# Five load buffers for the expert weights, with transposed halves in shared buffers and both silus first

## The chip, the cores and the metric

The kernel runs on one core of one Trainium2 chip. The metric is the device time of one execution in microseconds; lower is better. The names used below are those of the profile: PE is TensorE (matmuls), ACT is ScalarE, DVE is VectorE, POOL is GpSimd, SP is SyncE, whose queue issues nearly all plain DMA transfers.

## What is computed

One layer of a diffusion backbone over 2048 tokens of 1024 channels: a gated short convolution, and then a mixture of 16 experts in which each expert chooses its own 256 tokens. Cut to the part that the change touches:

```python
def expert_choice_ffn(h, w_router, w_gate, w_up, w_down):
    cap = EC_CAPACITY_FACTOR * N // N_EXPERTS                       # 256
    aff = jax.nn.softmax((h @ w_router).astype(jnp.float32), axis=-1)
    g, idx = lax.top_k(jnp.swapaxes(aff, 1, 2), cap)
    xs = jax.vmap(lambda hb, ib: hb[ib])(h, idx)
    hid = jax.nn.silu(einsum('becd,edf->becf', xs, w_gate)) * einsum('becd,edf->becf', xs, w_up)
    ys = einsum('becf,efd->becd', hid, w_down) * g[..., None]
    # rows of ys are added to the output at idx
```

Everything is float32. The expert weights are 16 x 3 x 1024 x 1024 numbers, 201 MB, each read once.

## The kernel before

The convolution part takes the first 800 us or so, then the router and a first search for the thresholds of experts 0 and 1, and from about 857 us on the experts, which the change is about. All of it is one program written out in Python; each engine executes its own instructions strictly in the order in which they are written, and the kernel sets that order by hand.

**Weights.** They come in pieces of 512 KB (`pieces`, 128 partitions x 1024 numbers). `load_piece` (L181) takes a buffer of the tag `raw`, of which there are `n_raw` = 3, and issues the load on SP's queue. `split_high` copies the piece, rounded to TensorE's float32r, into the first half of a `ws` buffer on ScalarE (L200); `split_low` subtracts that from the piece into the second half, on VectorE (L210). With the low half done the `raw` buffer is free, and the load of the piece three places on is issued (`load_to(i + n_raw)`). There are eight `ws` buffers (`n_split`); one comes free when the matmuls have used it.

**Products.** Three matmuls make one product in float32 precision: high by high, high by low, low by high. `gate_up(e, fh)` computes one half of the hidden channels of expert `e` for the gate and the up weights (192 matmuls of 256 columns, L1047, L1049 and L1051, into four PSUM banks), in eight steps `k`; `between(k)` places other work in them. Its eviction is a silu on ScalarE (L1057), a multiply on VectorE (L1058), a copy to the high half of `hT` on ScalarE (L1060) and a subtraction for the low half on VectorE (L1061), for each of two pairs of banks. `down(e, dh)` computes half of the output channels (48 matmuls of 512 columns, L1069 to L1071, two banks, four steps `kk`), evicted at L1089 and added into the output by an indirect DMA (L1095). Six banks are shared in turn, so a `gate_up` waits for the eviction of the `gate_up` before it. The order over experts is `gate_up(e, 0)`, `down(e-1, 0)`, `gate_up(e, 1)`, `down(e-1, 1)`.

**The tokens of the next expert.** `pick_oh` builds one-hot masks on VectorE (`oh`), `pick` multiplies them to the list of token numbers and issues two row gathers on POOL (L987) into two `xs` buffers, 128 rows each, whose float32 numbers lie as two halves of 16 bits. `turn(e, s)` transposes the rows of one half of the tokens by a DMA on SP's queue (L1015) into `tr`. `join(e, s)` puts the 16-bit halves together in `full` (VectorE L1021, ScalarE L1022) and splits that into `xT`, high on ScalarE (L1025), low on VectorE (L1026). The next expert's first matmul needs all of `xT`. In the kernel before, both turns and both joins stand inside `gate_up(e, 1)`, at k = 1, 3 and 5, 7.

Of the kernel before, what the change touches and what calls it, by code (L numbers as in the profile page):

```python
# [7 lines left out]
F32 = mybir.dt.float32  # L8
# [3 lines left out]
U16 = mybir.dt.uint16  # L12
# [5 lines left out]
P = 128  # L18
D = 1024
L = 2048  # L20
E = 16
CAP = 256
KD = D // P
# [13 lines left out]
def dram(src, offset, ap):  # L37
    return bass.AP(tensor=src.tensor, offset=src.offset + offset, ap=ap)
# [3 lines left out]
def block_kernel(ctx: ExitStack, tc, x, c, ada_w, ada_b, norm_g, w_in, conv, w_out, router, wg, wu, wd, out):  # L42
# [3 lines left out]
    wpool = ctx.enter_context(tc.tile_pool(name="weights", bufs=1))  # L46
# [3 lines left out]
    n_raw, n_split = 3, 8  # L50
# [121 lines left out]
    pieces, n_load, n_high, n_done = [], 0, 0, 0  # L172
# [3 lines left out]
        pieces.append((src, offset, ap, shape))  # L176
        return len(pieces) - 1

    raws = {}

    def load_piece(i):  # L181
        src, offset, ap, shape = pieces[i]
        t = wpool.tile([P] + shape, F32, name="raw", tag="raw", bufs=n_raw)
        nc.sync.dma_start(t, dram(src, offset, ap))
        raws[i] = t

# [2 lines left out]
    def load_to(i):  # L189
        nonlocal n_load  # L190
        while n_load <= min(i, len(pieces) - 1, load_end[0] - 1):
            load_piece(n_load)
            n_load += 1
# [10 lines left out]
    def split_low(i, eng=None, part=0, n=1):  # L204
        nonlocal n_done
        split_high(i)
        t, raw = ws_of[i], raws[i]
        w = pieces[i][3][-1] // n
        s = slice(part * w, (part + 1) * w)
        (eng or nc.vector).tensor_sub(t[:, 1, ..., s], raw[..., s], t[:, 0, ..., s].bitcast(F32))  # L210
        if part == n - 1:
            raws.pop(i)
            n_done += 1
            load_to(i + n_raw)

    def split_to(i, eng=None):
        while n_done <= min(i, len(pieces) - 1):
# [737 lines left out]
    moe = ctx.enter_context(tc.tile_pool(name="moe", bufs=1, reuse_waits="tile"))  # L955
# [16 lines left out]
    def pick(e):  # L972
        oh, ax = oh_of.pop(e)
        pi = tp.tile([P, 2, 5], F32, name="pi", tag="tp")
        for b in range(NB):
            nc.tensor.matmul(pi, oh[:, b], ax[:, b], start=(b == 0), stop=(b == NB - 1))
        pk = small.tile([P, 2, 5], F32, name="pk", tag="pk", bufs=2)
        nc.vector.tensor_copy(pk, pi)
        idx = small.tile([P, 2], I32, name="idx", tag="idx", bufs=4)
        nc.vector.scalar_tensor_tensor(idx, pk[:, :, 1], float(P), pk[:, :, 0], op0=ALU.mult, op1=ALU.add)  # L980
        xs_of[e] = []
        for s in range(2):
            if e:
                xs, src = moe.tile([P, 2 * D], U16, name="xs", tag="xs", bufs=2), hhalf.rearrange("t h d -> t (h d)")
            else:
                xs, src = moe.tile([P, D], F32, name="xs", tag="xs", bufs=2), hscr
            nc.gpsimd.indirect_dma_start(  # L987
                out=xs, out_offset=None, in_=src,
                in_offset=bass.IndirectOffsetOnAxis(ap=idx[:, s:s + 1], axis=0))
            xs_of[e].append(xs)  # L990
        gate = small.tile([P, 2], F32, name="gate", tag="gate", bufs=4)
        nc.vector.tensor_add(gate, pk[:, :, 2], pk[:, :, 3])
        nc.vector.tensor_add(gate, gate, pk[:, :, 4])
        idx_of[e], gate_of[e] = idx, gate

    def fetch(e, i, bank=None):
        g, s = divmod(i, 2)
        if i == 0:
            xT_of[e] = moe.tile([P, 2, KD, CAP], F32R, name="xT", tag="xT", bufs=2)
        xT, xs = xT_of[e], xs_of[e][s]  # L1000
        pt = (bank or tp).tile([P, 4, P], F32, name="pt", tag="mm" if bank else "tp")
        for j in range(4):
            nc.tensor.transpose(pt[:, j], xs[:, (4 * g + j) * P:(4 * g + j + 1) * P], identf)
        d = (slice(None), slice(4 * g, 4 * g + 4), slice(s * P, (s + 1) * P))
        nc.scalar.activation(xT[:, 0][d], pt, AF.Copy)
        nc.vector.tensor_sub(xT[:, 1][d], pt, xT[:, 0][d].bitcast(F32))

    tr_of = {}

    def turn(e, s):  # L1010

        if s == 0:
            xT_of[e] = moe.tile([P, 2, KD, CAP], F32R, name="xT", tag="xT", bufs=2)
        tr = tr_of[e, s] = moe.tile([P, 2 * KD, P], U16, name="tr", tag="oh" if s else "tr", bufs=1)
        nc.sync.dma_start_transpose(tr, xs_of[e][s])  # L1015

    def join(e, s):
        tr = tr_of.pop((e, s)).rearrange("p (h k) t -> p h (k t)", h=2)
        full = moe.tile([P, KD * P], F32, name="full", tag="full", bufs=1)
        both = full.bitcast(U16).rearrange("p (n h) -> p h n", h=2)  # L1020
        nc.vector.tensor_copy(both[:, 0], tr[:, 0])  # L1021
        nc.scalar.activation(both[:, 1], tr[:, 1], AF.Copy)  # L1022
        f = full.rearrange("p (k t) -> p k t", t=P)
        hi, lo = (xT_of[e][:, i, :, s * P:(s + 1) * P] for i in range(2))
        nc.scalar.activation(hi, f, AF.Copy)  # L1025
        nc.vector.tensor_sub(lo, f, hi.bitcast(F32))  # L1026

    def gate_up(e, fh, between=lambda k: None):
        xT = xT_of[e]
        if fh == 0:  # L1030
            hT_of[e] = {}
        ps = [[mm.tile([P, 2, CAP], F32, name="pm", tag="mm") for _ in range(2)] for _ in range(2)]
        for kk in range(KD // 2):
            for j in range(2):
                k = 2 * kk + j
                n = w_moe[0, e, fh, kk] + n_split - 2 + j
                if (e, fh) != (0, 1):
                    split_high(n)
                between(k)
                while n_done <= min(n, len(pieces) - 1):  # L1040
                    split_low(n_done, nc.gpsimd if n_done % 2 and (e, fh) < (1, 1) else None)
                for f in range(4):
                    c0 = slice(f * P, (f + 1) * P)
                    for m in range(2):
                        o = ps[m][f // 2][:, f % 2]
                        w = ws_of[w_moe[m, e, fh, kk]]
                        nc.tensor.matmul(o, w[:, 0, j, c0], xT[:, 0, k], start=(k == 0 and f % 2 == 0), stop=False,  # L1047
                                         skip_group_check=True)
                        nc.tensor.matmul(o, w[:, 0, j, c0], xT[:, 1, k], start=False, stop=False,  # L1049
                                         skip_group_check=True)  # L1050
                        nc.tensor.matmul(o, w[:, 1, j, c0], xT[:, 0, k], start=False, stop=(k == KD - 1),  # L1051
                                         skip_group_check=True)
        hT = moe.tile([P, 2, 4, CAP], F32R, name="hT", tag="hT", bufs=4)
        hT_of[e][fh] = hT
        for f2 in range(2):
            sg = moe.tile([P, 2, CAP], F32, name="sg", tag="sg", bufs=2)
            nc.scalar.activation(sg, ps[0][f2], AF.Silu)  # L1057
            nc.vector.tensor_mul(sg, sg, ps[1][f2])  # L1058
            t = slice(2 * f2, 2 * f2 + 2)
            nc.scalar.activation(hT[:, 0, t], sg, AF.Copy)  # L1060
            nc.vector.tensor_sub(hT[:, 1, t], sg, hT[:, 0, t].bitcast(F32))  # L1061
# [44 lines left out]
    def tick(k):  # L1106
        next(rounds, None)
# [8 lines left out]
    pick_oh(1)  # L1116
    for i in (0, 2, 1, 3):
        fetch(0, i, mm)
    for e in range(E):
        if e == 0:  # L1120
            gate_up(0, 0, lambda k: (tick(k), pick(1) if k == 7 else None))
            gate_up(0, 1, lambda k: (tick(k), turn(1, k - 2)) if k in (2, 3) else join(1, k - 5) if k in (5, 6) else None)
            continue
        if e == 1:
            gate_up(1, 0, lambda k: tick(k) if k > 1 else None)
            down(0, 0, lambda kk: tick(kk) if kk else None)
            for _ in rounds:
                pass
            pick_oh(2)
            gate_up(1, 1, lambda k: pick(2) if k == 2 else turn(2, k - 6) if k > 5 else None)  # L1130
        else:
            if e + 1 < E:
                pick_oh(e + 1)
            gate_up(e, 0)
            down(e - 1, 0, (lambda kk: pick(e + 1) if kk == 1 else None) if e + 1 < E else (lambda kk: None))
            gate_up(e, 1, (lambda k: turn(e + 1, k // 2) if k in (1, 3) else join(e + 1, k // 2 - 2) if k in (5, 7) else None)
                    if e + 1 < E else (lambda k: None))
        if e == 1:
            down(e - 1, 1, lambda kk: join(2, kk - 1) if kk in (1, 2) else None)
        else:  # L1140
            down(e - 1, 1)
    down(E - 1, 0)
    down(E - 1, 1)

# [21 lines left out]
```

## Time and profile before

| | |
|---|---|
| median of 3 runs | 2000.06 us (1997.33 to 2007.17) |
| the profiled execution | 2000.56 us, span 1998.8 us |
| mean granted TensorE clock | 0.978 |
| PE busy | 94% of the span |
| DVE, ACT, POOL busy | 58%, 41%, 17% |
| DMA moved | 368.50 MB, mean 184 GB/s |
| the sixteen experts | from about 857 us to the end |

In the profile's rows the first number is a start in microseconds from the start of the span, the second a duration; a group's row ends with the idle time before it and what ended that idle time. A windows row gives the length of a stretch, then for each engine its busy time and its number of instructions, then the granted clock, the busy share of the DMA engines and GB/s. A waits row gives who waited for whom: total, times, longest. Line numbers are those of the kernel before. A matmul's recorded end is modelled, and consecutive ones overlap.

### The profile page before, as it was taken

The numbers are of one execution on the slowest core, as the hardware profiler recorded it, in microseconds if no ns is written. First come the engines' busy times: TensorE is split into PE (matmuls) and PEld (weight loads), VectorE is DVE, ScalarE is ACT, GpSimd is POOL, SyncE is SP. The second block draws the span as 40 slices with busy tenths as digits, with TensorE's granted clock in tenths as the row PEclk, the third lists the DMA queues.
The fourth block names the chain that finished last, engine by engine and source line by source line (L and its number), as shares of the span: only waits on it lengthen the run. The fifth ranks groups of instructions, "written<-read, shape, count | busy, mean of one in ns | idle before, by whom it ended". The sixth has DMA issues, their size and how long they took to land.

```text
span 1998.8 us, 29375 instructions
## 1 busy us (share of the span) xinstructions
PE 1885.4 (94%) x11690; PEld 1659.4 (83%) x11690; DVE 1151.3 (58%) x1656; ACT 820.8 (41%) x1066; POOL 343.7 (17%) x521
## 2 busy tenths in 40 slices
PE   4999999999999999289999999999999999999998
PEld 3788888888888888288899989889898988988896
DVE  7644435344346667877656665665665656566554
ACT  3421126111123444456444454554445445454442
POOL 3310011010112223433102102101200110211101
PEclk9999999999999999589999999999999999999999
DMA  9343241433245565346777878778677777867866
GB/s 283 124 148 132 69 142 51 150 136 117 69 132 173 190 196 190 137 140 194 210 237 218 214 220 247 207 220 234 203 223 229 232 216 223 239 197 229 244 203 155
DMA packets 281278, 368.50 MB, mean 184 GB/s; under 512 B 74748, under 2 KB 156724, under 8 KB 281140
## 3 DMA queue, kind: packets, MB, share of 16 engines
q1 hardware_dynamic: 265172, 308.94, 50.5%
q0 software_dynamic: 15968, 57.68, 10.8%
q8 instruction: 91, 1.49, 0.3%
q14 instruction: 47, 0.39, 0.1%
HBM read 300.51 MB, written 50.33 MB: 176 GB/s over the span
## 4 chain that ended last, share of the span: by engine, by line
PE 58%; DMA 14%; DVE 12%; issue 7%; ACT 6%; SPq 2%; POOL 1%; POOLq 0%; ACTq 0%; DVEq 0%
PE pm L439 8%; PE pm L440 8%; PE pm L442 8%; PE pm L1051 5%; PE pm L1047 5%; PE pm L1049 5%; DVE ws L210 4%; DMA raw<-in_moe_w_gate_dram 4%; DMA raw<-in_moe_w_down_dram 4%; ACT ws L200 3%; DMA raw<-in_moe_w_up_dram 3%; PE pm L644 3%; PE pm L647 3%; PE pm L645 3%; PE pm L1071 2%
## 5 line engine op out<-in xcount | busy, mean ns | idle before, releaser
L210 DVE TENSOR_TENSOR ws<-raw,ws 128x1024 fp32r<-128x1024 f32 x415 | 499.6, 1225 | 315.6 <-ACT ws L200 312.2
L200 ACT ACTIVATE ws<-raw 128x1024 fp32r<-128x1024 f32 x437 | 452.7, 1055 | 459.8 <-DMA raw<-in_moe_w_down_dram 202.0
L1047 PE MATMUL pm<-xT,ws 128*128 128x256 f32 x2048 | 580.1, 283 | 21.2 <-DVE sg L1058 14.7
L1049 PE MATMUL pm<-xT,ws 128*128 128x256 f32 x2048 | 575.2, 281 | 5.2 <-DVE xT L1026 4.9
L1051 PE MATMUL pm<-xT,ws 128*128 128x256 f32 x2048 | 574.2, 280 | 2.5 <-DVE ws L210 2.5
L1047 PEld LDWEIGHTS pm<-xT,ws 128*128 128x128 f32 x2048 | 392.1, 191 | 30.6 <-DVE sg L1058 19.3
L1049 PEld LDWEIGHTS pm<-xT,ws 128*128 128x128 f32 x2048 | 391.8, 191 | 9.0 <-DVE xT L1026 7.8
L1051 PEld LDWEIGHTS pm<-xT,ws 128*128 128x128 f32 x2048 | 391.9, 191 | 3.8 <-DVE ws L210 3.7
L439 PE MATMUL pm<-hl,ws 128*128 128x512 f32 x768 | 305.2, 397 | 0.9 <-ACT hl L389 0.9
L440 PE MATMUL pm<-hl,ws 128*128 128x512 f32 x768 | 301.3, 392 | 0.0
L442 PE MATMUL pm<-hl,ws 128*128 128x512 f32 x768 | 217.7, 392 | 0.0
L1095 POOL DMA_INDIRECT out_dram<-ot,idx x32 | 101.2, 3163 | 636.9 <-DVE ot L1089 626.6
L1071 PE MATMUL pm<-ws,hT 128*128 128x512 f32 x512 | 201.5, 394 | 0.0
L1070 PE MATMUL pm<-ws,hT 128*128 128x512 f32 x512 | 200.6, 392 | 0.7 <-DVE ws L210 0.7
L1069 PE MATMUL pm<-ws,hT 128*128 128x512 f32 x512 | 201.2, 393 | 0.0
L439 PEld LDWEIGHTS pm<-hl,ws 128*128 128x128 f32 x768 | 145.5, 189 | 31.7 <-ACT hl L389 1.3
L442 PEld LDWEIGHTS pm<-hl,ws 128*128 128x128 f32 x768 | 145.4, 189 | 30.7
L440 PEld LDWEIGHTS pm<-hl,ws 128*128 128x128 f32 x768 | 145.5, 190 | 30.4 <-issue 1.0
L452 DVE TENSOR_TENSOR u<-cs,pm 128x512 f32<-128x512 f32 x32 | 22.5, 703 | 231.4 <-ACT cs L449 231.4
L449 ACT ACTIVATE cs<-pm 128x512 f32<-128x512 f32 x32 | 19.1, 598 | 332.1 <-issue 261.2
L1070 PEld LDWEIGHTS pm<-ws,hT 128*128 128x128 f32 x512 | 96.2, 188 | 21.7 <-DVE ws L210 1.6
L1071 PEld LDWEIGHTS pm<-ws,hT 128*128 128x128 f32 x512 | 96.2, 188 | 20.4
(273 smaller groups left out, 2073.3 us busy)
## 6 DMA issues: line engine op xcount, KB each, us to landing
raw<-in_moe_w_gate_dram SPq DMA_DIRECT2D x128, 512.0 KB
raw<-in_moe_w_up_dram SPq DMA_DIRECT2D x128, 512.0 KB
raw<-in_moe_w_down_dram SPq DMA_DIRECT2D x128, 512.0 KB
raw<-in_sc_w_in_dram SPq DMA_DIRECT2D x45, 512.0 KB
xt<-in_x_dram SPq DMA_DIRECT2D x32, 512.0 KB
aw<-in_ada_w_dram SPq DMA_DIRECT2D x32, 512.0 KB
hl<-in_ada_w_dram SPq DMA_DIRECT2D x32, 256.0 KB
hl<-vscr SPq DMA_DIRECT2D x16, 512.0 KB
```

Source lines behind the costliest of these rows:

```text
L200: nc.scalar.activation(t[:, 0], raws[n_high], AF.Copy)
L210: (eng or nc.vector).tensor_sub(t[:, 1, ..., s], raw[..., s], t[:, 0, ..., s].bitcast(F32))
L439: nc.tensor.matmul(ps[m], wh, t[:, 0], start=(k == 0), stop=False)
L440: nc.tensor.matmul(ps[m], wl, t[:, 0], start=False, stop=False)
L442: nc.tensor.matmul(ps[m], W(k, m)[0], t[:, 1], start=False, stop=(k == KD - 1))
L1047: nc.tensor.matmul(o, w[:, 0, j, c0], xT[:, 0, k], start=(k == 0 and f % 2 == 0), stop=False, skip_group_check=True)
L1049: nc.tensor.matmul(o, w[:, 0, j, c0], xT[:, 1, k], start=False, stop=False, skip_group_check=True)
L1051: nc.tensor.matmul(o, w[:, 1, j, c0], xT[:, 0, k], start=False, stop=(k == KD - 1), skip_group_check=True)
L1069: nc.tensor.matmul(ps[s], h, w[:, 0, j], start=(k == 0), stop=False)
L1070: nc.tensor.matmul(ps[s], h, w[:, 1, j], start=False, stop=False)
L1071: nc.tensor.matmul(ps[s], l, w[:, 0, j], start=False, stop=(k == KD - 1))
L1095: st = nc.gpsimd.indirect_dma_start(out=out_rows, out_offset=bass.IndirectOffsetOnAxis(ap=idx_of[e][:, s:s + 1], axis=0), in_=ots[s], in_o ...
```

## The change

Four edits. From the experts on, `raw` has two more buffers in the experts' pool (`more`), taken in turn with the three, so loads run five pieces ahead. The space comes from the tags `tr` and `full`, which go: the transposed halves of the first 128 tokens lie in the one-hot buffer `oh`, those of the second in a row buffer `xs`, and the joined rows `full` the other way round. With this the turns of experts 3 and on stand at k = 2 and 4 of `gate_up(e, 1)`, the first join at k = 7 and the second at kk = 1 of the following `down(e-1, 1)`; for experts 1 and 2 the steps move by one. Last, an eviction's two silus and two multiplies come ahead of its two copies and two subtractions.

```diff
+    raws, more = {}, []
+    def depth():
+        return n_raw + (2 if more else 0)
     def load_piece(i):
-        t = wpool.tile([P] + shape, F32, name="raw", tag="raw", bufs=n_raw)
+        if more and more[1] % (n_raw + 2) < 2:
+            t = more[0].tile([P] + shape, F32, name="raw", tag="raw", bufs=2)
+        else:
+            t = wpool.tile([P] + shape, F32, name="raw", tag="raw", bufs=n_raw)
+        if more:
+            more[1] += 1
         nc.sync.dma_start(t, dram(src, offset, ap))
...
-            load_to(i + n_raw)
+            load_to(i + depth())
...
-        tr = tr_of[e, s] = moe.tile([P, 2 * KD, P], U16, name="tr", tag="oh" if s else "tr", bufs=1)
+        tr = tr_of[e, s] = moe.tile([P, 2 * KD, P], U16, name="tr", tag="xs" if s else "oh", bufs=2 if s else 1)
...
-        full = moe.tile([P, KD * P], F32, name="full", tag="full", bufs=1)
+        full = moe.tile([P, KD * P], F32, name="full", tag="oh" if s else "xs", bufs=1 if s else 2)
...
-        for f2 in range(2):
-            sg = moe.tile([P, 2, CAP], F32, name="sg", tag="sg", bufs=2)
+        sgs = [moe.tile([P, 2, CAP], F32, name="sg", tag="sg", bufs=2) for _ in range(2)]
+        for f2, sg in enumerate(sgs):
             nc.scalar.activation(sg, ps[0][f2], AF.Silu)
             nc.vector.tensor_mul(sg, sg, ps[1][f2])
+        for f2, sg in enumerate(sgs):
             t = slice(2 * f2, 2 * f2 + 2)
             nc.scalar.activation(hT[:, 0, t], sg, AF.Copy)
             nc.vector.tensor_sub(hT[:, 1, t], sg, hT[:, 0, t].bitcast(F32))
...
+    more[:] = [moe, 0]
+    load_to(n_done + depth() - 1)
     for e in range(E):
         if e == 0:
-            gate_up(0, 1, lambda k: (tick(k), turn(1, k - 2)) if k in (2, 3) else join(1, k - 5) if k in (5, 6) else None)
+            gate_up(0, 1, lambda k: (tick(k), turn(1, k - 2)) if k in (2, 3) else join(1, k - 6) if k > 5 else None)
...
-            gate_up(1, 1, lambda k: pick(2) if k == 2 else turn(2, k - 6) if k > 5 else None)
+            gate_up(1, 1, lambda k: pick(2) if k == 1 else turn(2, k - 5) if k in (5, 6) else None)
...
-            gate_up(e, 1, (lambda k: turn(e + 1, k // 2) if k in (1, 3) else join(e + 1, k // 2 - 2) if k in (5, 7) else None)
+            gate_up(e, 1, (lambda k: turn(e + 1, k // 2 - 1) if k in (2, 4) else join(e + 1, 0) if k == 7 else None)
...
-            down(e - 1, 1)
+            down(e - 1, 1, (lambda kk: join(e + 1, 1) if kk == 1 else None) if e + 1 < E else (lambda kk: None))
```

How this moves the instructions: on SP's queue, around one expert's two transposes, before:

```order
L184 DMA raw<-in_moe_w_gate_dram 128x2x512
L184 DMA raw<-in_moe_w_up_dram 128x2x512
L184 DMA raw<-in_moe_w_down_dram 128x2x512 x2
L1015 DMA_TRANSPOSE tr<-xs 128x16x128
L184 DMA raw<-in_moe_w_down_dram 128x2x512 x2
L1015 DMA_TRANSPOSE tr<-xs 128x16x128
L184 DMA raw<-in_moe_w_gate_dram 128x2x512
```

and after:

```order
L192 DMA raw<-in_moe_w_down_dram 128x2x512 x4
L192 DMA raw<-in_moe_w_gate_dram 128x2x512
L1023 DMA_TRANSPOSE tr<-xs 128x16x128
L192 DMA raw<-in_moe_w_up_dram 128x2x512
L192 DMA raw<-in_moe_w_gate_dram 128x2x512
L1023 DMA_TRANSPOSE tr<-xs 128x16x128
L192 DMA raw<-in_moe_w_up_dram 128x2x512
```

The transposes now stand three loads further down the row of loads, with two loads between them as before.

On ScalarE, from the last splits of an expert's second half over its eviction into the next expert (`ws<-raw` is a split, `full<-tr` and `xT<-full` a join, `sg<-pm` a silu, `hT<-sg` a copy), before:

```order
L200 ACTIVATE ws<-raw 128x1024 x10
L1022 ACTIVATE full<-tr 128x1024
L1025 ACTIVATE xT<-full 128x8x128
L200 ACTIVATE ws<-raw 128x1024 x2
L1022 ACTIVATE full<-tr 128x1024
L1025 ACTIVATE xT<-full 128x8x128
L1057 ACTIVATE sg<-pm 128x512
L1060 ACTIVATE hT<-sg 128x512
L1057 ACTIVATE sg<-pm 128x512
L1060 ACTIVATE hT<-sg 128x512
L200 ACTIVATE ws<-raw 128x1024 x12
```

and after:

```order
L208 ACTIVATE ws<-raw 128x1024 x12
L1030 ACTIVATE full<-tr 128x1024
L1033 ACTIVATE xT<-full 128x8x128
L1065 ACTIVATE sg<-pm 128x512 x2
L1069 ACTIVATE hT<-sg 128x512 x2
L208 ACTIVATE ws<-raw 128x1024 x2
L1030 ACTIVATE full<-tr 128x1024
L1033 ACTIVATE xT<-full 128x8x128
L208 ACTIVATE ws<-raw 128x1024 x10
```

The first join moves behind two more splits, the second behind the eviction and two more splits, and the two silus stand together.

More of the change, by code (lines that the diff above doesn't have):

```diff
@@ L177, in add_piece @@
         return len(pieces) - 1
-    raws = {}
+    raws, more = {}, []
+    def depth():
+        return n_raw + (2 if more else 0)
     def load_piece(i):
         src, offset, ap, shape = pieces[i]
-        t = wpool.tile([P] + shape, F32, name="raw", tag="raw", bufs=n_raw)
+        if more and more[1] % (n_raw + 2) < 2:
[4 more added lines that the diff above has]
+            more[1] += 1
         nc.sync.dma_start(t, dram(src, offset, ap))
```

## The prediction

> **What bounds the kernel now.** First the page's engine shares, then stretches of one expert each.
>
> ```profile
> span 1998.8 us, 29375 instructions
> PE 1885.4 (94%) x11690; PEld 1659.4 (83%) x11690; DVE 1151.3 (58%) x1656; ACT 820.8 (41%) x1066; POOL 343.7 (17%) x521
> ```
>
> TensorE looks full, but its matmuls overlap in the records, so the share hides small losses. The table of windows shows them: each row runs from the first matmul of one expert's second gate/up half to that of the next expert's, with the same matmuls in each; thirteen such rows, of which the first three and the sum:
>
> ```profile
> core 0: us, PE busy (x) PEld busy (x) DVE busy (x) ACT busy (x) POOL busy (x), PEclk, DMA share, GB/s
> 1025.30:1091.36 66.06, 66.06 (x497) 61.91 (x496) 41.26 (x48) 32.48 (x35) 8.01 (x4) 1.00 0.75 216
> 1091.36:1157.42 66.06, 66.06 (x497) 61.91 (x496) 39.22 (x43) 31.11 (x34) 10.20 (x5) 1.00 0.83 234
> 1157.42:1226.38 68.96, 67.62 (x498) 62.81 (x497) 42.70 (x49) 33.27 (x35) 10.61 (x5) 1.00 0.77 226
> ...
> sum 908.39, PE 883.35 PEld 818.50 DVE 551.55 ACT 434.97 POOL 125.90; mean PE 67.95 PEld 62.96 DVE 42.43 ACT 33.46 POOL 9.68
> ```
>
> Two experts take 66.06 us with TensorE never idle; the other eleven take (908.39 - 2 x 66.06) / 11 = 70.6 us. Against 13 x 66.06 the loss is 49.6 us, and VectorE, the busiest of the others, works 42 us of 70. The same table by stages shows where it sits:
>
> ```profile
> 988.23:1013.79 25.56, 24.88 (x192) 24.58 (x193) 16.43 (x18) 9.79 (x11) 5.35 (x3) 0.87 0.77 219
> 1091.36:1113.14 21.78, 21.78 (x194) 21.77 (x192) 10.86 (x11) 9.76 (x9) 2.59 (x2) 1.00 1.06 289
> 1113.14:1124.13 10.99, 10.99 (x51) 9.02 (x50) 7.84 (x10) 6.98 (x9) 0.00 (x0) 1.00 0.53 176
> 1330.47:1356.19 25.72, 24.11 (x192) 23.61 (x193) 17.74 (x21) 10.22 (x12) 7.62 (x3) 0.93 0.70 199
> 1332.80:1336.20 3.40, 3.23 (x15) 3.23 (x16) 2.01 (x4) 2.38 (x4) 0.00 (x0) 0.50 0.55 157
> ```
>
> A gate/up half without loss is 21.78 us, a down half 10.99. The first half of a late expert (the row at 1330) takes 25.72, and near its start TensorE's granted clock is 0.50 for 3.4 us. The waits from 1020 to 1940, of TensorE, of the load queue on SP and of ScalarE (total, times, longest):
>
> ```profile
> PE pm L1047 <- DVE sg L1058: 14.7, 18, 1.2
> PE pm L1047 <- ACT sg L1057: 3.6, 6, 1.6
> ...
> SPq L184 <- DVE ws L210: 576.2, 269, 5.1
> ...
> ACT ws L200 <- DMA raw<-in_moe_w_down_dram: 180.6, 96, 8.3
> ACT ws L200 <- DMA raw<-in_moe_w_up_dram: 138.0, 75, 3.8
> ```
>
> TensorE waits for PSUM banks that an eviction (`sg`) has not emptied. SP waits for a split to free a `raw` buffer; the split waits for the load. That loop with three buffers is the bound, and the eviction is late because it stands behind such splits. ScalarE and VectorE at the start of the half that begins at 1330.47, in order of time:
>
> ```profile
> 1326.05 1.06 ACT L200 ACTIVATE ws<-raw 128x1024 fp32r<-128x1024 f32 x1 [0.24 <-DMA raw<-in_moe_w_up_dram]
> 1327.01 1.36 ACT L1022 ACTIVATE full<-tr 128x1024 uint16<-128x1024 uint16 x1
> 1328.87 1.06 ACT L1025 ACTIVATE xT<-full 128x1024 fp32r<-128x1024 f32 x1 [0.50 <-DVE full L1021]
> 1329.84 0.58 ACT L1057 ACTIVATE sg<-pm 128x512 f32<-128x512 f32 x1
> 1332.95 0.63 ACT L1060 ACTIVATE hT<-sg 128x512 fp32r<-128x512 f32 x1 [2.54 <-DVE sg L1058]
> ```
>
> ```profile
> 1328.04 0.74 DVE L1021 COPY full<-tr 128x1024 uint16<-128x1024 uint16 x1
> 1329.96 1.23 DVE L1026 TENSOR_TENSOR xT<-full,xT 128x1024 fp32r<-128x1024 f32 x1 [1.18 <-ACT xT L1025]
> 1331.11 1.22 DVE L210 TENSOR_TENSOR ws<-raw,ws 128x1024 fp32r<-128x1024 f32 x1
> 1332.24 0.68 DVE L1058 TENSOR_TENSOR sg<-sg,pm 128x512 f32<-128x512 f32 x1
> 1333.62 0.69 DVE L1061 TENSOR_TENSOR hT<-sg,hT 128x512 fp32r<-128x512 f32 x1 [0.70 <-ACT hT L1060]
> ```
>
> The first silu of the half before last runs at 1329.84, a whole down half late. What stretches the loop most is the pair of transposes on the load queue (SP's timeline, then one load as the chain that ended last has it):
>
> ```profile
> 1309.57 4.12 SPq L1015 DMA_TRANSPOSE tr<-xs  x1
> 1313.78 1.48 SPq L184 DMA_DIRECT2D raw<-in_moe_w_down_dram  x2
> 1315.36 5.42 SPq L1015 DMA_TRANSPOSE tr<-xs  x1
> ...
> 1338.94 4.70 DMA raw<-in_moe_w_gate_dram
> ```
>
> **Five buffers.** An expert has 24 pieces of weights: 70.6 / 24 = 2.94 us a piece, times three buffers 8.8 us a turn of the loop, made of the load 4.70, high half 1.06, low half 1.22, and 1.8 of queueing. With five and the same turn, supply takes 24 x 8.8 / 5 = 42 us an expert; if a load stretches with the number in flight (4.70 x 5 / 3 = 7.8), 24 x 11.9 / 5 = 57. The DMA engines' own limit is their share, 0.77 x 70.6 = 54 us of work. All lie under 66.06. In rates: 226 GB/s x 68.96 us, spread over 66.06, is 236 GB/s, and the stage at 1091 ran 289. A transpose holds SP 4.1 to 5.4 us, up to two pieces at 66.06 / 24 = 2.75; five buffers cover that, three barely. So TensorE becomes the bound and the 49.6 us go. The last expert's first half lies outside the thirteen rows; it has a stall of its own, which I leave out of the sum.
>
> **Silus first.** Before, the second silu stood behind the first copy, which waited 2.54 us for VectorE. Now the second multiply, which frees a bank, follows the first directly, earlier by a copy and a subtraction, 0.63 + 0.69 us. With the eviction on time the down half hides this, so the sum has nothing for it; were supply still late, it would shorten each stall by up to 1.3 us, 11 x 1.3 = 14 us.
>
> **Joins moved, halves in shared buffers.** No instruction is added. Two waits are: the second transpose overwrites the rows that the first one reads, so SP waits for the first to land, with weight loads queued behind; and the first join writes over the second rows, so it waits for the second transpose. For the landing, the early pair on SP and its first user on ScalarE, and the row gathers' landing:
>
> ```profile
> 895.52 4.08 SPq L1015 DMA_TRANSPOSE tr<-xs  x1
> ...
> 901.81 1.39 ACT L1022 ACTIVATE full<-tr 128x1024 uint16<-128x1024 uint16 x1
> ...
> DMA to landing us min/median/max: 6.2/7.2/8.6
> ```
>
> So at most 6.3 us from issue to use there. Let a second half start at 0; its eight k-steps take 2.72 us each, and pieces are split in pairs when TensorE passes 0, 5.4, 10.9 and 16.3. The first transpose goes at about 3.9 (rows gathered, the split ahead done at 3.5) and lands at 10.2; the second follows and lands near 17. The first join stands behind two splits, 16.3 + 0.3 + 2 x 1.06 = 18.7, so 1.7 us cover it. VectorE ends that join and its last split near 23.5, the multiplies 24.8; ScalarE ends the copies 25.5 and two splits 27.4; VectorE's splits end 28.8, the second join's copies 29.6, its high half 30.7, its low half 32.0. The next expert's first matmul is due at 21.78 + 10.99 = 32.8: 0.8 us of cover, thin. The bounds: nothing if it holds; if every expert stalls 1.5 us, 13 x 1.5 = 20, and with the 3.4 us at half clock behind each stall (1.7 lost) 42. I take 0.5 us an expert, 6 us, near the lower end, since each chain still closes.
>
> The Trainium skill, "TensorE: Matmul & The Clock Gate", Part 1 on the HAM clock gate, has the clock halve after an idle window of some 3.4 us; by that a stall of 1.5 us would cost itself alone, 20 us in all instead of 42. The rows disagree: no wait of TensorE here is longer than 1.6 us, and the clock is 0.50 at 1332.80.
>
> **The start of the experts.** In expert 0 the second transpose now waits until 901.8, so the joins, begun at 901.81 before, wait until about 901.8 + 6.3 = 908, and expert 1 starts perhaps 3 us later. Against that, expert 2's first half (25.56 at 988.23, 3.8 over 21.78) loses in the same way as the late ones and may be mended. Together -1 us, between +5 and -8.
>
> **Sum.** The profiled execution took 2000.56 us (its span and 1.8 around it); the median of the runs is 2000.06. 2000.56 - 49.6 - 1 + 6 = 1956, rounded to 1955. Half a per cent, 10 us, is about what a measurement here can tell from no change.
>
> **Rivals.** A is the forecast: 1946 to 1962, chance 0.58.
>
> E: the joins cost nothing and the early stages gain in full, 1955 - 6 - 7 = 1942. For it, ScalarE's waits for loads; against, the early stages also carry the routing search. 0.10.
>
> B: the joins become the wait. The second transpose or the second join slips past its cover, and each expert stalls at its first matmul; 7 to 36 us more than the 6 counted, 1962 to 1991. For it, covers of 1.7 and 0.8 us; against, nothing on these engines would then wait for loads. 0.20.
>
> C: five buffers don't do what they say, since more loads in flight only land later (the share of 1.06 at 1091 is a full DMA system). Half or less of the 49.6 returns: 1975 to 2000. Against, 0.77 on average. 0.08.
>
> D, slower: the join wait again, but long, because SP's hold for the first landing delays the second transpose and starves the splits with it. It decides once the second join ends 3 us behind its 32.0, since 13 x (2.2 + 1.7) takes back 50 us; at 5 us behind it is 13 x (4.2 + 1.7) - 49.6 = 27 slower, about 2027. It needs the buffers to run dry: a hold of some 11 us is four pieces of five. 0.04.
>
> The range 1942 to 1984 holds A, most of B and part of E and C, about 0.8. Faster by over 0.5% (under 1990): A, E, nearly all of B, half of C, 0.90; the same 0.06; slower 0.04.
>
> **What would show it.** Right: stretches of 66 to 67 us an expert throughout at clock 1.00, ScalarE's waits for the three kinds of loads a fraction of what they were, splits waiting for TensorE instead. Wrong: a first half whose matmuls wait for `xT` (B, D), or for `sg` with splits still waiting for loads (C). The forecast fails if loads land much later than 7.8 us, or the second transpose later than 19 us into its half.

## The result, and the profile after

The changed kernel takes 1944.79 us (median of 4 runs, 1941.42 to 1946.39) against 1999.32 for the kernel before, run beside it (4 runs, 1997.33 to 2007.17). The ratio is 0.9718, with a 95% interval of 0.9689 to 0.9747. The forecast was 1955, between 1942 and 1984. The medians differ by 54.5 us. The profiled execution took 1941.42 us, just under the forecast's range; that is 59.1 less than the one profiled before, and it is the fastest of the four.

First the shares of the engines and the chain of work that ended last, by engine, from the page of the changed kernel, and then the chain of the kernel before:

```profile
span 1939.6 us, 29422 instructions
PE 1853.9 (96%) x11690; PEld 1640.7 (85%) x11690; DVE 1145.1 (59%) x1656; ACT 810.5 (42%) x1066; POOL 349.9 (18%) x521
...
PE 90%; DVE 3%; DMA 2%; SPq 1%; issue 1%; ACT 1%; POOL 1%; POOLq 0%; ACTq 0%; DVEq 0%
```

```profile
PE 58%; DMA 14%; DVE 12%; issue 7%; ACT 6%; SPq 2%; POOL 1%; POOLq 0%; ACTq 0%; DVEq 0%
```

The share of PE has risen by two points only, but the chain now lies on TensorE for 90% of the span, where it was 58%. Next the stretches of one expert each, cut as in the prediction: first and last of the thirteen rows, the first half and the following down half of the expert that had stalled at 1330, the 3.4 us that had run at half clock, and the sum of the thirteen:

```profile
core 0: us, PE busy (x) PEld busy (x) DVE busy (x) ACT busy (x) POOL busy (x), PEclk, DMA share, GB/s
1017.65:1083.71 66.06, 66.06 (x498) 61.91 (x497) 42.88 (x50) 33.23 (x36) 10.50 (x5) 1.00 0.84 241
1810.37:1875.90 65.53, 65.53 (x481) 61.59 (x480) 39.82 (x41) 33.22 (x36) 3.25 (x3) 1.00 0.81 234
sum 858.25, PE 858.25 PEld 804.57 DVE 554.32 ACT 432.06 POOL 129.16; mean PE 66.02 PEld 61.89 DVE 42.64 ACT 33.24 POOL 9.94
```

```profile
1314.65:1336.43 21.78, 21.78 (x193) 21.78 (x192) 14.70 (x17) 7.95 (x10) 7.63 (x3) 1.00 0.91 266
1336.43:1347.95 11.52, 11.52 (x67) 9.34 (x66) 8.60 (x13) 6.58 (x8) 2.87 (x2) 1.00 0.64 222
1332.80:1336.20 3.40, 3.40 (x32) 3.40 (x31) 2.15 (x3) 0.67 (x2) 0.00 (x0) 1.00 0.81 289
```

Twelve experts in a row take 66.06 us (one 66.05, one 66.07), all at clock 1.00; the last row ends where the last expert has no successor. Against 908.39 that is 50.1 us. The waits from 1012 on say why. ScalarE's longest entries, then SP's first:

```profile
ACT ws L208 <- PE pm L1059: 293.9, 81, 4.1
ACT ws L208 <- PE pm L1080: 50.7, 30, 1.7
ACT sg L1065 <- PE pm L1059: 46.9, 41, 2.1
```

```profile
SPq L192 <- DVE ws L218: 611.0, 283, 5.7
```

The 377 us that ScalarE had waited for the three kinds of loads (180.6, 138.0 and, for the gate weights, 58.6) are gone altogether; it now waits for TensorE to use up `ws` buffers (L208 is the split that was L200). SP still waits for splits, as it did, but no wait for a load of weights is left on ScalarE or VectorE, and the list of the waits of TensorE's matmuls from 1012 to the end is empty.

### The profile page after: what moved, and what is told of

The parts are those of the page before. It is cut to its first block, busy times and chain, and to the rows that moved or that the text cites. A ratio compares the mean times of both kernels' runs of the same rounds, so it can differ in the third digit from the quotient of the medians.

```text
span 1939.6 us, 29422 instructions
## 1 busy us (share of the span) xinstructions
PE 1853.9 (96%) x11690; PEld 1640.7 (85%) x11690; DVE 1145.1 (59%) x1656; ACT 810.5 (42%) x1066; POOL 349.9 (18%) x521
## 4 chain that ended last, share of the span: by engine, by line
PE 90%; DVE 3%; DMA 2%; SPq 1%; issue 1%; ACT 1%; POOL 1%; POOLq 0%; ACTq 0%; DVEq 0%
PE pm L1055 11%; PE pm L1057 11%; PE pm L1059 11%; PE pm L447 9%; PE pm L448 9%; PE pm L450 9%; PE pm L1080 6%; PE pm L1078 6%; PE pm L1079 6%; PE pm L652 3%; PE pm L653 3%; PE pm L655 3%; DMA tr<-xs 1%; SPq L410 1%; DVE hl L322 1%
## 5 line engine op out<-in xcount | busy, mean ns | idle before, releaser
L218 DVE TENSOR_TENSOR ws<-raw,ws 128x1024 fp32r<-128x1024 f32 x415 | 494.5, 1225 | 275.2 <-ACT ws L208 275.1
L208 ACT ACTIVATE ws<-raw 128x1024 fp32r<-128x1024 f32 x437 | 441.1, 1051 | 401.2 <-PE pm L1059 320.1
L1055 PE MATMUL pm<-xT,ws 128*128 128x256 f32 x2048 | 568.4, 278 | 3.0 <-ACT xT L1033 3.0
L1057 PE MATMUL pm<-xT,ws 128*128 128x256 f32 x2048 | 566.9, 277 | 2.1 <-DVE xT L1034 1.7
L1059 PE MATMUL pm<-xT,ws 128*128 128x256 f32 x2048 | 566.5, 277 | 0.0
L1055 PEld LDWEIGHTS pm<-xT,ws 128*128 128x128 f32 x2048 | 385.2, 188 | 4.7 <-ACT xT L1033 3.5
L1057 PEld LDWEIGHTS pm<-xT,ws 128*128 128x128 f32 x2048 | 385.6, 188 | 4.0 <-DVE xT L1034 2.1
L1059 PEld LDWEIGHTS pm<-xT,ws 128*128 128x128 f32 x2048 | 385.1, 188 | 0.0
L1104 POOL DMA_INDIRECT out_dram<-ot,idx x32 | 108.1, 3377 | 603.2 <-DVE ot L1098 599.2
```

What stands on the lines that cost most here:

```text
L208: nc.scalar.activation(t[:, 0], raws[n_high], AF.Copy)
L1104: st = nc.gpsimd.indirect_dma_start(out=out_rows, out_offset=bass.IndirectOffsetOnAxis(ap=idx_of[e][:, s:s + 1], axis=0), in_=ots[s], in_o ...
```

## Where the 59 us came from

The table compares the two profiled executions.

| stretch | before | after | gain |
|---|---|---|---|
| expert 2's second half to expert 15's second half | 908.39 | 858.25 | 50.1 |
| expert 0's second down half and expert 2's first half | 39.56 | 34.30 | 5.3 |
| the rest up to expert 2's second half | 985.74 | 983.35 | 2.4 |
| expert 15's second half to the end | 65.1 | 63.7 | 1.4 |

For the second row, the windows of the changed kernel; before they were 14.00, from 974.23 to 988.23, and 25.56:

```profile
971.84:983.10 11.26, 11.26 (x50) 8.88 (x48) 8.06 (x10) 9.14 (x11) 0.00 (x0) 1.00 0.73 220
983.10:1006.14 23.04, 22.17 (x194) 21.97 (x193) 16.26 (x18) 9.58 (x11) 7.62 (x3) 1.00 0.86 245
```

The 50.1 us can be taken apart with the waits of TensorE's weight loads in the kernel before, which stand ahead of the matmuls' own (from 1020 on):

```profile
PEld pm L1047 <- DVE sg L1058: 19.1, 21, 1.4
PEld pm L1047 <- ACT sg L1057: 6.8, 7, 2.1
PEld pm L1049 <- DVE xT L1026: 5.7, 10, 0.6
PEld pm L1051 <- DVE ws L210: 3.7, 6, 1.6
...
PEld pm L1070 <- DVE ws L210: 1.6, 2, 1.0
```

They add up to 36.9 us. Six stretches of 3.4 us at half clock, the one at 1332.80 among them, each lose 1.7 us, together 10. That makes 47 of the 50. In three of the first halves, at 1190.19, 1259.14 and 1472.99, the matmuls follow each other every 118 ns instead of 113, some 0.8 us in a half; why, these runs don't show. After the change the only entry left in this list is 3.3 us that belongs to the masks of the next expert's tokens, which was there before too.

## The experiments

The theory was the prediction's: the loop of loads through three buffers is the bound, depth removes it, the pair of transposes stretches the loop most, and the order of the silus is worth little. The rivals were that the order of the silus does the work, that the transposes matter little, and that the covers of the joins are not thin at all. The runs, each against the kernel before of its own call (median 2003.11, 2003.51 and 2000.93 us in the three calls):

| kernel | buffers | silus first | halves and joins | median us | ratio (95%) |
|---|---|---|---|---|---|
| silus only | 3 | yes | as before | 1964.36 | 0.9806 (0.9787, 0.9825) |
| all but the depth | 3 | yes | moved | 1983.30 | 0.9892 (0.9859, 0.9924) |
| plain loads for transposes | 3 | no | as before | 1989.42 | 0.9937 (0.9917, 0.9957) |
| all but the silus | 5 | no | moved | 1945.83 | 0.9719 (0.9700, 0.9737) |
| four buffers | 4 | yes | moved | 1943.33 | 0.9703 (0.9684, 0.9721) |
| second join later | 5 | yes | moved | 1960.40 | 0.9780 (0.9757, 0.9802) |
| own transposed buffer | 4 | yes | nearly as before | 1942.02 | 0.9705 (0.9689, 0.9720) |
| the change again | 5 | yes | moved | 1944.44 | 0.9715 (0.9700, 0.9731) |

**All but the depth.** The changed kernel with three buffers.

```diff
-    more[:] = [moe, 0]
-    load_to(n_done + depth() - 1)
```

> The changed kernel with three load buffers again; shared buffers, moved joins and silus first stay. Theory (depth): the load loop is the bound again, an expert takes about 70 us and the time is 1980 to 2000. Rival (order): the moved joins and the silus let the eviction run on time, and three buffers are enough: 1945 to 1955. In between, up to 1.3 us of each stall may go with the silus: 1980 to 1986.

It took 1983.30 us (1976.20 to 1993.55). TensorE's waits from 1020 on, in the slowest of the four:

```profile
PE pm L1055 <- ACT xT L1033: 13.7, 7, 3.5
PE pm L1057 <- DVE xT L1034: 8.9, 11, 0.9
```

Without the depth the moved joins become the wait: every entry is for `xT`. The joins stand behind splits, and ScalarE's splits wait for loads again, 295 us from 1020 to 1880. The two extra buffers are worth some 39 us on top of the rest of the change (1983.30 - 1944.79).

**Silus only.** The kernel before, with both silus and multiplies ahead of the copies and subtractions.

```diff
-        for f2 in range(2):
-            sg = moe.tile([P, 2, CAP], F32, name="sg", tag="sg", bufs=2)
+        sgs = [moe.tile([P, 2, CAP], F32, name="sg", tag="sg", bufs=2) for _ in range(2)]
+        for f2, sg in enumerate(sgs):
...
+        for f2, sg in enumerate(sgs):
```

> The kernel before with the two silus and multiplies first, nothing else. Theory (depth): the stalls at an expert's first half shrink by at most 1.3 us and their half-clock stretch by up to 1.7, over eleven experts: 1967 at the least, rather 1985 to 1998, since the loads still set the pace. Rival (order): the late eviction was the cause itself, and most of the 50 us go: 1950 to 1965.

It took 1964.36 us, 39 below the kernel before: a swap of order does two thirds of what the whole change does, and without the moved joins and shared halves three buffers are 19 us faster than with them (1983.30 - 1964.36). The profiled execution is the slowest of its five, 1973.79; its thirteen experts take 882.60 us against 908.39, 25.8 less, which probably understates the gain. ScalarE's waits from 1020 to 1880, of the kernel before and then of this one:

```profile
ACT ws L200 <- DMA raw<-in_moe_w_down_dram: 165.1, 89, 8.3
ACT ws L200 <- DMA raw<-in_moe_w_up_dram: 134.2, 71, 3.8
ACT hT L1060 <- DVE sg L1058: 68.1, 48, 2.5
```

```profile
ACT ws L200 <- DMA raw<-in_moe_w_down_dram: 154.4, 84, 5.4
ACT ws L200 <- DMA raw<-in_moe_w_up_dram: 127.5, 71, 4.9
...
ACT hT L1061 <- DVE sg L1058: 37.7, 25, 2.1
```

The hold of ScalarE in the eviction, its copy waiting for VectorE's multiply with all later splits queued behind it, falls from 68.1 to 37.7 us. The waits for loads fall little; a split still waits for its load. That the shorter hold makes the gain is not shown, though it is of about that size: the swap also changes when the banks come free, and the waits of TensorE's weight loads say more. From 1020 to 1940 they are now:

```profile
PEld pm L1051 <- DVE ws L210: 11.0, 15, 1.5
...
PEld pm L1047 <- ACT sg L1057: 2.9, 3, 1.8
PEld pm L1049 <- DVE xT L1026: 2.7, 6, 0.6
PEld pm L1047 <- DVE sg L1058: 0.4, 1, 0.4
PEld pm L1071 <- DVE ws L210: 0.3, 1, 0.3
```

The 25.9 us of waits for evictions (`sg`) have become 3.3, and those for weights have risen from 5.3 to 11.3. In all 19.6 us of waits are gone, and five of the six stretches at half clock (8.5 us); together that is 28 us, near the 25.8 of the profile. The largest part of the 25.9, 15.7 us in twelve halves, stood ahead of a half's fourth matmul, the first for the up weights: in the kernel before it writes the bank that the first multiply empties, and that multiply stands behind a join and a split on VectorE. In the program with the new order, the first half of an expert has for this matmul the bank that the second silu empties. The kernel before, in the half that begins at 1330.47, and then this one, in the half that begins at 1530.11:

```profile
1332.97 0.58 PE L1047 MATMUL pm<-xT,ws 128*128 128x256 f32 x1 [1.23 <-DVE sg L1058]
```

```profile
1531.22 0.28 PE L1047 MATMUL pm<-xT,ws 128*128 128x256 f32 x1
1531.88 1.28 DVE L1058 TENSOR_TENSOR sg<-sg,pm 128x512 f32<-128x512 f32 x2
```

The matmul that waited for the first multiply now goes ahead of it. So most of the waits that are gone were for banks that now come free earlier. The waits for the first silu and for `xT` shrink too, from 12.5 to 5.6 us together; whether that comes of the shorter hold stays open.

**All but the silus.** The changed kernel with the old order of the eviction.

> The changed kernel with the silus as before (silu, multiply, copy, subtract, pair by pair). Theory (depth): the next expert's tokens end 1.6 us ahead of their first matmul in the changed kernel's trace; the old order delays the second join by about 1 us or less, so TensorE still never idles in steady state: 1941 to 1950, early stages included. Rival (order): the cover is used up, each of 13 experts stalls 0.5 to 2 us: 1952 to 1990.

It took 1945.83 us (1945.50 to 1947.33), 1 us from the changed kernel's median. Its thirteen experts, in one window:

```profile
1021.99:1880.24 858.25, 858.25 (x6433) 804.56 (x6432) 554.33 (x629) 429.68 (x468) 124.40 (x63) 1.00 0.81 239
```

ScalarE's hold is back in it (65.4 us in 52 waits, near the kernel before) and costs nothing: with five buffers no split and no eviction is late enough for TensorE to wait. So the 39 us of the silus and the 57 us that this kernel gains without them (2003.11 - 1945.83) do not add: both pay for the same stalls, and depth pays for all of them. No run has the depth without the moved joins and shared halves, which make its room; with three buffers these cost 19 us.

**Four buffers.** One buffer more instead of two.

```diff
-        return n_raw + (2 if more else 0)
+        return n_raw + (1 if more else 0)
-        if more and more[1] % (n_raw + 2) < 2:
-            t = more[0].tile([P] + shape, F32, name="raw", tag="raw", bufs=2)
+        if more and more[1] % (n_raw + 1) < 1:
+            t = more[0].tile([P] + shape, F32, name="raw", tag="raw", bufs=1)
```

> The changed kernel with four load buffers. Theory (depth, by the turn of 8.8 us): 24 x 8.8 / 4 = 53 us an expert, under 66.06, so four are enough: 1941 to 1952. Rival (two transposes hold the queue too long for four, or a load stretches): an expert takes 67 to 69 us in the middle: 1955 to 1975.

It took 1943.33 us (1942.60 to 1945.78), with 858.26 us for the thirteen experts. The fifth buffer is worth nothing that these runs can tell.

**Second join later.** The second join at kk = 3 instead of kk = 1, behind two more splits.

```diff
-            down(e - 1, 1, (lambda kk: join(e + 1, 1) if kk == 1 else None) ...)
+            down(e - 1, 1, (lambda kk: join(e + 1, 1) if kk == 3 else None) ...)
```

> The changed kernel with the second join at kk = 3 of the down half instead of kk = 1, so two more splits stand ahead of it on ScalarE and VectorE. Theory (cover): the tokens end 1.6 us ahead of their first matmul now; two splits of 1.14 us on VectorE use that up, and each of 13 experts stalls about 0.7 us, with or without a half-clock stretch of 1.7: 1953 to 1976. Rival (the join is far from the path): no change, 1941 to 1948.

It took 1960.40 us (1955.40 to 1964.08). The thirteen experts, and the one wait of the matmuls from 1020 on:

```profile
1021.97:1897.63 875.66, 869.46 (x6433) 812.00 (x6432) 555.16 (x629) 431.07 (x468) 102.18 (x63) 1.00 0.80 234
```

```profile
PE pm L1057 <- DVE xT L1034: 6.2, 13, 0.5
```

An expert loses (875.66 - 858.25) / 13 = 1.34 us on average, most of it in its first half, whose first matmuls with the low half of `xT` wait for the join: 10.3 us of the 17.4 in the waits of the weight loads, at most 0.9 at a time. Most of the rest lies in nine halves, three of them second halves without a wait, whose matmuls follow each other every 118 ns instead of 113; the cause is open. So the cover of the join in the changed kernel is real and short: two splits more use it up.

**Two thirds of the products.** Two kernels, the changed one and the one before, leave out the high-by-low matmuls of the experts, so that TensorE has a third less work there and the supply shows. Both were run once.

> The changed kernel without the high-by-low matmuls of the experts (two of three products are left, so the result is less exact); TensorE then needs about 44 us an expert and supply is the bound. Theory (five buffers carry 42 to 57 us, the DMA engines 54): an expert takes 50 to 57 us. Rival (supply was only just enough): 60 us or more.

> The kernel before without the high-by-low matmuls of the experts (two of three products are left). Theory (three buffers are the bound by themselves): an expert still takes 69 to 71 us. Rival (the loop of three is stretched by the engines' own order, evictions and joins, which wait for TensorE): with TensorE faster the same loop turns faster, 60 to 67 us.

With five buffers it took 1811.04 us, with three 2017.90. The stretches are expert 2's second half to the end of twelve experts for the first, and eleven experts for the second:

```profile
1026.78:1737.24 710.46, 562.85 (x4033) 524.60 (x4033) 513.25 (x589) 402.62 (x433) 149.42 (x60) 0.88 0.91 267
```

```profile
1110.39:1913.52 803.13, 612.13 (x3696) 529.33 (x3697) 475.49 (x540) 372.33 (x396) 114.33 (x55) 0.88 0.77 216
```

That is 59.2 and 73.0 us an expert, the first between what was expected of theory and rival, the second above both. With three buffers and the old order the experts take no less time although TensorE has a third less to do, so it was not TensorE that set the pace there; evictions and joins are part of this loop, and its mean clock of 0.88 says that TensorE ran at half clock for a quarter of the stretch. With five, supply carries an expert in 59.2 us or less, since there the matmuls wait for the next expert's tokens and not for weights:

```profile
PE pm L1055 <- ACT xT L1033: 157.4, 13, 13.8
```

**Plain loads for transposes.** The kernel before, with a plain load of the same size in the place of each transpose; the experts from 1 on then work on other tokens' numbers.

```diff
-        nc.sync.dma_start_transpose(tr, xs_of[e][s])
+        nc.sync.dma_start(tr, hhalf[s * P:(s + 1) * P].rearrange("t h (k d) -> t (h k) d", d=P))
```

> The kernel before with each DMA transpose replaced by a plain load of the same size from the table of token rows, so the experts from 1 on work on other tokens' numbers. It takes the 4.4 us holds of SP's queue away and leaves three buffers. Theory (the holds stretch the loop): a turn falls from 8.8 to 7.4 us or so, 24 x 7.4 / 3 = 59 us, under 66.06, and most of the loss goes: 1945 to 1960. Rival (three buffers are the bound anyway): 1980 to 2000.

It took 1989.42 us (1984.94 to 1992.14), 14 below the kernel before. SP is now held for half a microsecond in the place of 4.12 and 5.42 (its timeline near 1300):

```profile
1301.98 0.56 SPq L1015 DMA_DIRECT2D tr<-hhalf  x1
1307.63 0.46 SPq L1015 DMA_DIRECT2D tr<-hhalf  x1
```

```profile
ACT hT L1060 <- DVE sg L1058: 73.8, 52, 2.5
```

With the holds of SP gone, ScalarE's hold in the eviction is what it was, and so are most of the stalls: the thirteen experts take 895.87 us, 12.5 less than before. From 1020 to 1940 SP had also waited 46 us in 21 waits ahead of its transposes, for TensorE and for the gathered rows; it doesn't wait ahead of the plain loads, so the 12.5 us are the worth of both. The transposes stretched the loop, but not most. Without them the early loss goes too: expert 0's second down half and expert 2's first half take 11.82 and 23.02 us here, much as in the changed kernel.

**Own transposed buffer, and the change again.** Four buffers, silus first, and the first transpose in a buffer of its own again, so that neither the second transpose waits for the first nor the first join for the second; the joins of expert 1 one step earlier.

```diff
-        tr = tr_of[e, s] = moe.tile([P, 2 * KD, P], U16, name="tr", tag="xs" if s else "oh", bufs=2 if s else 1)
+        tr = tr_of[e, s] = moe.tile([P, 2 * KD, P], U16, name="tr", tag="oh" if s else "tr", bufs=1)
-        full = moe.tile([P, KD * P], F32, name="full", tag="oh" if s else "xs", bufs=1 if s else 2)
+        full = moe.tile([P, KD * P], F32, name="full", tag="xs", bufs=2)
```

> Four load buffers, silus first, and the transposed halves where they were in the kernel before (one in a buffer of its own, one in the one-hot buffer); only the joined rows share the two row buffers, each over the rows that its own transpose has read, so neither SP nor a join gets a new wait. Joins of expert 1 back at k = 5 and 6. Theory: the 3 us that expert 1's first matmul waited more in the changed kernel come back and nothing else moves: 2 to 4 us under the changed kernel of this call. Rival: expert 1 waits for the search anyway: within 1 us of it.

> The changed kernel again, beside the one with its own transposed buffer: 1941 to 1947, with no wait of TensorE from expert 2 on.

They took 1942.02 us (1941.63 to 1943.84) and 1944.44 (1943.66 to 1945.87), five runs each. The wait of expert 1's first matmul, with the buffer of its own and then in the changed kernel:

```profile
PE pm L1055 <- ACT xT L1033: 0.9, 1, 0.9
```

```profile
PE pm L1055 <- ACT xT L1033: 3.6, 1, 3.6
```

The 2.7 us that the shared buffers cost at expert 1 come back, and the medians differ by 2.4. The first has the lowest median of the study, though the ranges of the two overlap by 0.2 us, and by its ratio to the kernel before of its own call (0.9705) it is no faster than four buffers with the shared halves (0.9703).

## Why the prediction was right, and where it was not

- **The bound, -49.6: right for the order before.** 50.1 us came back, with every expert at the 66.06 us that the trace before showed for two. The term is the whole loss, so its size alone would fit any cure of the stalls; that depth is enough, the runs with four buffers and with the old order show. That the loop with three buffers is the bound at 70.6 us holds for the old order alone: with the silus first three buffers took 882.60 / 13 = 67.9 us an expert on average, against 908.39 / 13 = 69.9. Supply with five buffers, put at 42 to 57 us an expert, was not measured exactly; 59.2 in the kernel with two thirds of the products is an upper end, and lies under 66.06. Loads did not stretch to 7.8 us: their medians from issue to landing are 5.1, 4.6 and 4.8 us for gate, up and down.
- **The joins, +6: mis-sized.** They cost nothing. The cover was put at 0.8 us. VectorE and the first matmul of the next expert, in the timeline of the second half that starts at 1281.89:

```profile
1307.71 2.36 DVE L218 TENSOR_TENSOR ws<-raw,ws 128x1024 fp32r<-128x1024 f32 x2 [0.26 <-ACT ws L208]
1309.98 0.77 DVE L1029 COPY full<-tr 128x1024 uint16<-128x1024 uint16 x1
1311.94 1.23 DVE L1034 TENSOR_TENSOR xT<-full,xT 128x1024 fp32r<-128x1024 f32 x1 [1.19 <-ACT xT L1033]
```

```profile
1314.65 0.28 PE L1055 MATMUL pm<-xT,ws 128*128 128x256 f32 x1
```

  The low half ends at 1313.17, 31.3 us into the half where 32.0 was worked out, and the matmul is due at 32.8, as worked out: 1.5 us of cover. The chain was right and 0.7 us too long, and on a cover of 0.8 that is the difference between a term and none. Charging half a microsecond to every expert for a cover that was positive by the working itself was the mistake. That the cover is thin was right, as the later join shows.
- **The start, -1: mis-sized.** The extra wait at expert 1 was put at 3 us; it is 3.0 in this profile and 3.6 in the second one, and 2.7 of these came back with a buffer of its own. But the loss in expert 2's first half was booked for only part of its 3.8, and expert 0's second down half, 14.00 us before, was not looked at. Both recover for the most part in each kernel with four or five buffers, 5.3 us here. The last expert's first half and the end, named as left out, gave another 1.4. The other 2.4 us of the start are no steady gain: in the second profile of the changed kernel, expert 2's second half starts at 1020.57, 2.9 us later than in the first.
- **"What stretches the loop most is the pair of transposes": wrong.** Without them, and without SP's waits ahead of them, 12.5 us of the 50 came back in that profile.
- **"Silus first", nothing in the sum: right; at most 14 us if supply were late: wrong.** With three buffers they are worth 39. The step priced the earlier second multiply, 1.3 us a stall in the eleven experts with one. But the second multiply accounts for only 3.4 us of TensorE's 25.9 for evictions; 15.7 hung on the first multiply, and the swap took these away since the matmul behind them got another bank. Nor did the step count the half clock that goes with the waits, 8.5 us. That ScalarE's hold of up to 2.5 us also stood in the load loop, in both halves of every expert, is likely but not shown.
- **Rivals.** E, joins free and the early gain in full, 1942, came nearer than the forecast A, which the median misses by 1 us at its lower end. The median lies 10 us under the 1955 of the sum and 3 us above the range's lower end, which stands where E does. B and D, the joins as the wait, occurred only with three buffers or with a later join. C did not.
- **The clock.** The rule weighed in the prediction, from the Trainium skill, "TensorE: Matmul & The Clock Gate", Part 1, would have a stall of 1.5 us cost itself alone. The later join agrees, with stalls of 0.9 us at most: no stretch of its experts ran below full clock. The kernel before agrees only in part: none of its waits in the experts exceeds 2.1 us, and six stretches ran at half clock. But the prediction looked at single waits. In the half at 1330.47 three of them follow each other with three matmuls between, and in the 3.41 us ahead of 1332.81 TensorE is busy for 1.33; the last section has the rest.

## What to carry to other kernels

Before a late eviction is priced, find which matmul waits, for which bank, and what empties that bank: here the largest wait hung on one multiply behind a join and a split, and a new order of four instructions took it away by giving that matmul another bank. Holds of an engine that executes in order, and waits that follow each other closely, belong into the sum beside the transfer and the work on it. Two edits that pay for the same stall do not add, so run each alone before crediting either; here one more buffer was enough, and the cheapest edit, the swap, did two thirds with no memory at all. A cover that the rows show to be positive should be carried as zero cost with a risk beside it, not as a cost.

## What was not expected of the hardware

The granted clock falls to half in stretches of 3.41 us in the kernel before (at 1332.81, 1404.49, 1476.17, 1547.85, 1619.53 and 1759.48), after waits none of which is above 2.1 us, while the stalls of the later join set off none. The six starts lie 71.7 us apart, the last 140.0, which is 21 and 41 times 3.413 us: within an execution the clock changes on a fixed grid, and so it does in the other profiles. What tells the pieces of the grid apart that are followed by half clock is how busy TensorE was in them. Of the kernel before, the pieces ahead of 1332.81 and of 1759.48, and one at 1827.74 behind which the clock stayed full:

```profile
1329.40:1332.81 3.41, 1.33 (x5) 0.49 (x4) 2.85 (x3) 1.02 (x2) 0.00 (x0) 1.00 0.60 229
1756.07:1759.48 3.41, 1.79 (x13) 1.54 (x13) 2.71 (x5) 1.12 (x2) 0.00 (x0) 1.00 0.46 146
1827.74:1831.15 3.41, 2.00 (x14) 1.55 (x13) 2.69 (x4) 1.12 (x2) 0.00 (x0) 1.00 0.39 136
```

In the four profiles with all three products and such stretches from 1020 to 1935 (this one, silus only, plain loads, all but the depth) each of the thirteen stretches follows a piece at full clock with 1.8 us or less of busy TensorE, and no such piece with 2.0 us or more is followed by one. With two thirds of the products both outcomes occur between 1.5 and 2.0 us, so the border is not sharp in this measure. The least busy piece among the experts of the later join has 2.87 us. So several short waits close together can cost half clock, and where the grid falls decides: the halves at 1755.70 and 1826.69 have much the same waits at their start, and only the first is followed by a stretch.

An SP transpose of 128 x 2048 numbers of 16 bits held SP's queue for 4.12 and 5.42 us, where a plain load of the same size held it for 0.56 and 0.46.
